# The sample tokens' depthwise convolution as products on GpSimd and sums on VectorE

## The chip, the cores and the metric
The kernel runs on one core of one Trainium2 chip. The metric is the device time of one execution in microseconds (us). A core has a matrix engine (TensorE, PE in the profile, with its weight loads as PEld), VectorE (DVE), ScalarE (ACT), GpSimd (POOL) and SyncE (SP), which here only issues DMAs. Each engine runs its own row of instructions strictly in order, and waits on semaphores for what other engines produce.

## The reference
One layer of a streaming encoder: a half-step SwiGLU feed-forward network, a mixer, a second half-step network, a norm. 1024 prompt tokens and 8 sample requests of 16 tokens pass through the same weights. The mixer projects each token once into q, k, v, eight forget logits and the two halves of a GLU:

```
z = h @ w_in                              # q | k | v | forget logits | conv GLU pair
q, k = rms(q) * g_q, rms(k) * g_k         # per head of 64
logf = log_sigmoid(fl + b_f)              # summed along time for the attention
u = a * sigmoid(gt)                       # 512 channels
y[t, c] = sum_j u_pad[t + j, c] * conv_w[j, c] + conv_b[c]     # 31 taps, causal
out = concat(attention(q, k, v, logf), silu(layernorm(y))) @ w_out
```

For the prompt, u_pad starts with 30 zeros; for each sample request it starts with 30 stored rows and has 16 new ones. The change concerns y of the 8 x 16 = 128 sample tokens alone.

## The kernel before
Channels lie on the 128 partitions, in four channel tiles (ct). For each of them, u[ct] holds 30 zeros and 1024 prompt columns, and behind them, as usv[ct], eight stretches of 46 columns, one for a request. acc[ct] has 1152 columns for y: 1024 of the prompt, 128 of the sample tokens. cw holds the 31 tap weights of each channel, convb (in vecs) the bias.

The mixer starts with the GLU: for each ct and each of three token chunks PE multiplies, ACT takes the sigmoid, DVE the product into u (the function glu). Then follows the projection, called the z stage here: six column blocks cb of 256 columns (the first with the 8 forget logits besides, 264), in the order v, v, k, k, q, q. A block takes nine tiles of 128 tokens, the sample tokens (tt = 8) first; a tile is 24 matmuls into a PSUM tile z. Weights come by DMA, are rounded on ACT (wh, L117), and the rest that was rounded off is taken on POOL (wl, L118); two such pieces belong to a block and are split two blocks ahead.

What happens to z of a tile depends on its block. In blocks 0 and 1 ACT copies it out; in block 0 DVE also adds the forget logits' bias (fl, L849). In blocks 2 to 5 ACT sums the squares of each head and takes the root, and DVE takes the reciprocal (rr, L858). In blocks 2 to 4 ACT copies z, POOL multiplies the copy by rr (L865), and for k by the gain as well (L869). In block 5 DVE multiplies z by rr straight from PSUM (L862). The sample rows stay on the chip as kts and qts, and PE transposes them five tiles later (q8T). z has six PSUM tiles in turn.

At the end of block 0 the log-sigmoid is computed for all tokens at once: two ACT operations and a chain of some twenty short DVE operations on 72 columns (ezq, L763 to L772, with lf as its result). In block 3, PE transposes lf, and DVE runs the cumulative sums as scans (nf L789; nfs L807, and L809 with 16 columns).

The convolution runs on DVE beside all this. The generator conv_taps goes through four ct of 31 taps; one step issues two operations: a tap on the prompt's 1024 columns, accumulated in PSUM (cv, L693 for the first tap, L696), and the same tap on the 128 sample columns, accumulated in acc (L694, L697). Five steps are taken after each GLU piece of ct 2 and 3, one or two after each tile of the z stage, the rest behind the loop.

PE's order is written by hand; the other engines' rows are ordered by a scheduler from the program's order, priorities and assumed costs. So code added at one place can shift instructions at many others. The attention, the layer norm, w_out and the second network follow the z stage.

Of the kernel before, what the change touches and what calls it, by code (L numbers as in the profile page):

```python
# [1 line left out]

# [10 lines left out]
ALU = mybir.AluOpType  # L13
AX = mybir.AxisListType
# [3 lines left out]
P = 128  # L18
D = 1024
KD = D // P  # L20
SEQ = 1024
NS = 8
TS = 16
# [9 lines left out]
CW = 31  # L33
# [10 lines left out]
def trunk_layer(  # L44
# [9 lines left out]
    pe, act, dve, pool_e, sp = nc.tensor, nc.scalar, nc.vector, nc.gpsimd, nc.sync  # L54
# [13 lines left out]
    def tmp(n, name="tmp", p=P):  # L68
        t = tp.tile([P, 768], F32, tag="tmp", name=name)
        return t[:p, :n]  # L70
# [7 lines left out]
    def defer(n, f):  # L78
        pending.append([n, f])

    def tick():
        for e in pending:
            e[0] -= 1
        due = [e for e in pending if e[0] <= 0]
        for e in due:
            pending.remove(e)
        for _, f in due:
            f()
# [91 lines left out]
    cw = const.tile([P, 4, CW], F32, name="cw")  # L180
# [9 lines left out]
    convb, lng, lnb = (vecs[:, 96 + 4 * i:100 + 4 * i] for i in range(3))  # L190
# [10 lines left out]
    def bank(name="b"):  # L201
        return ps.tile([P, 512], F32, tag="b", name=name, bufs=nb)
# [163 lines left out]
    def run(gen, n):  # L366
        for _ in range(n):
            if next(gen, "end") == "end":
                return False
        return True  # L370
# [274 lines left out]
    u = [up_.tile([P, ST + SEQ + NS * (ST + TS)], F32, tag=f"u{ct}", name=f"u{ct}") for ct in range(4)]  # L645
    acc = [up_.tile([P, NTOK], F32, tag=f"acc{ct}", name=f"acc{ct}") for ct in range(4)]
    usv = [t[:, ST + SEQ:].rearrange("p (s t) -> p s t", t=ST + TS) for t in u]
# [36 lines left out]

    def conv_taps():
        for ct in range(4):
            av = acc[ct][:, SEQ:].rearrange("p (s t) -> p s t", t=TS)
            cv = ps.tile([P, SEQ], F32, tag="cv", name="cv", bufs=1)
            for j in range(CW):
                w = cw[:, ct, j:j + 1]  # L690
                u0, u1 = u[ct][:, j:j + SEQ], usv[ct][:, :, j:j + TS]
                if j == 0:
                    dve.tensor_scalar(cv, u0, w, convb[:, ct:ct + 1], ALU.mult, ALU.add)  # L693
                    dve.tensor_scalar(av, u1, w, convb[:, ct:ct + 1], ALU.mult, ALU.add)  # L694
                else:
                    dve.scalar_tensor_tensor(cv if j < CW - 1 else acc[ct][:, :SEQ], u0, w, cv, ALU.mult, ALU.add)  # L696
                    dve.scalar_tensor_tensor(av, u1, w, av, ALU.mult, ALU.add)  # L697
                yield

    conv = conv_taps()  # L700

    def glu(ct, c, w0, w1):
        pa, pb = glu_mm(c, w0, w1)
        sg = tmp(C, "sg")
        act.activation(sg, pb[:, :C], AF.Sigmoid)
        n = C if c < 2 else 256
        dve.tensor_tensor(u[ct][:, ST + c * C:ST + c * C + n], pa[:, :n], sg[:, :n], ALU.mult)
        if c == 2:
            dve.tensor_tensor(
                usv[ct][:, :, ST:], pa[:, 256:C].rearrange("p (s t) -> p s t", t=TS),  # L710
                sg[:, 256:].rearrange("p (s t) -> p s t", t=TS), ALU.mult)
# [5 lines left out]
    for ct in range(2, 4):  # L717
        w = [ws.take(b_u + 2 * ct + i) for i in range(2)]
# [6 lines left out]
    def conv_states():  # L725
        t2 = tmp(DC, "us2")
        for ct in range(4):
            act.copy(t2[:, ct * P:(ct + 1) * P].rearrange("p (s t) -> p s t", t=TS), usv[ct][:, :, ST:])
        defer(2, lambda: conv_states_out(t2))
# [23 lines left out]
    def out_rows(flat, tt):  # L753
        return flat[0][tt * P:(tt + 1) * P] if tt < 8 else flat[1]

    def log_sigmoid():
        sh = [P, 72]
        x = fl.rearrange("p a b -> p (a b)")
        ezq = tmp(216, "ezq")
        e, z, q = (ezq[:, 72 * i:72 * i + 72] for i in range(3))  # L760
        act.activation(e, x, AF.Abs)
        act.activation(e, e, AF.Exp, scale=-1.0)
        dve.tensor_scalar(z, e, 2.0, None, ALU.add)  # L763
        dve.reciprocal(z, z)
        dve.tensor_tensor(z, z, e, ALU.mult)
        dve.tensor_tensor(e, z, z, ALU.mult)
        dve.tensor_scalar(q, e, 1.0 / 17, 1.0 / 15, ALU.mult, ALU.add)
        for d in (13, 11, 9, 7, 5, 3, 1):
            dve.tensor_tensor(q, q, e, ALU.mult)
            dve.tensor_scalar(q, q, 1.0 / d, None, ALU.add)  # L770
        dve.scalar_tensor_tensor(q, z, 2.0, q, ALU.mult, ALU.mult)
        dve.scalar_tensor_tensor(lf.rearrange("p a b -> p (a b)"), x, 0.0, q, ALU.min, ALU.subtract)  # L772
        sp.dma_start(f_prompt[0, 0].rearrange("(i p) h -> p i h", p=P), lf[:, 0:8, :])
        sp.dma_start(f_sample[0].rearrange("s t h -> (s t) h"), lf[:, 8, :])
# [41 lines left out]
    def sample_rows(cb):  # L816
        return (kts if cb < 4 else qts)[:, 2 * (cb % 2):2 * (cb % 2) + 2, :].rearrange("p a t -> p (a t)")

    def sample_t(cb):
        b = bank("q8T")  # L820
        dst = sample_rows(cb)
        for p in range(2):
            T(b[:, p * P:(p + 1) * P], dst[:, p * P:(p + 1) * P])
        if cb < 4:
            act.copy(dst, b[:, :256])
        else:
            act.activation(dst, b[:, :256], AF.Copy, scale=gqc)

    for cb, (c0, n) in enumerate(QKV):
        i0 = b_qkv + 2 * cb  # L830
        w = [ws.take(i0 + kq) for kq in range(2)]
        ws.split(i0 + 4)
        for tt in [8] + list(range(8)):
            c, o = divmod(tt, 3)
            b = bank("z")
            for kt in range(KD):
                a_h = hh[c][:, kt, o * P:(o + 1) * P]
                a_l = hl[c][:, kt, o * P:(o + 1) * P]
                wh, wl = (t[:, kt % 4, :] for t in w[kt // 4])
                pe.matmul(b[:, :n], lhsT=a_h, rhs=wh, start=kt == 0, stop=False)  # L840
                pe.matmul(b[:, :n], lhsT=a_h, rhs=wl, start=False, stop=False)
                pe.matmul(b[:, :n], lhsT=a_l, rhs=wh, start=False, stop=kt == KD - 1)
            cols = slice(c0 % DA, c0 % DA + 256)
            rows = slice(tt * P, (tt + 1) * P)
            t = sample_rows(cb) if tt == 8 and cb > 1 else tmp(256, "qkv")
            if cb < 2:
                act.copy(t, b[:, :256])
                if cb == 0:
                    dve.tensor_tensor(fl[:, tt, :], b[:, 256:264], bfb, ALU.add)  # L849
                sp.dma_start(out_rows(vflat, tt)[:, cols], t)  # L850
                sp.dma_start(vd[rows, cols], t)
            else:
                sq = up_.tile([P, DH], F32, tag="sq", name="sq", bufs=1)
                rr = up_.tile([P, 4], F32, tag="rr", name="rr", bufs=3)
                for h in range(4):
                    act.activation(sq, b[:, h * DH:(h + 1) * DH], AF.Square, accum_out=rr[:, h:h + 1])
                act.activation(rr, rr, AF.Sqrt, scale=1.0 / DH, bias=eps)
                dve.reciprocal(rr, rr)  # L858
                tv = t.rearrange("p (h d) -> p h d", h=4)
                rb = rr.unsqueeze(2).to_broadcast([P, 4, DH])  # L860
                if cb == 5:
                    dve.tensor_tensor(tv, b[:, :256].rearrange("p (h d) -> p h d", h=4), rb, ALU.mult)  # L862
                else:
                    act.copy(t, b[:, :256])
                    pool_e.tensor_tensor(tv, tv, rb, ALU.mult)  # L865
                if tt == 8:
                    defer(5, lambda cb=cb: sample_t(cb))
                if cb < 4:
                    pool_e.tensor_tensor(tv, tv, gkb.unsqueeze(1).to_broadcast([P, 4, DH]), ALU.mult)  # L869
                    sp.dma_start(out_rows(kflat, tt)[:, cols], t)  # L870
                if tt < 8:
                    sp.dma_start((kd if cb < 4 else qd)[rows, cols], t)
            run(conv, 1 + tt % 2)
            tick()
            if cb == 3:
                run(cum, 1)
        if cb == 0:
            log_sigmoid()
            conv_states()

    while run(conv, 1):
        pass

# [321 lines left out]
    for n in range(len(stages) + LAG):  # L1205
        q = {k: [] for k in "SBXY"}
        if n < len(stages):
            h, j = stages[n]
# [9 lines left out]
        if n >= LAG:  # L1218
            h, j = stages[n - LAG]
# [138 lines left out]
```

## Time and profile before
| | us |
|---|---|
| median of 3 runs | 2374.18 (2370.69 to 2375.71) |
| profiled execution, device time | 2371.12 |
| its span | 2369.4 |
| PE busy in the span | 2301.1 (97%) |
| DVE busy | 1240.5 (52%) |
| ACT busy | 654.3 (28%) |
| POOL busy | 532.9 (22%) |

The device time has 1.7 us outside the span. The busy shares are means over stages: in most of the program DVE is far from full, in the GLU and the z stage it isn't, which is to be read from windows of the trace. The z stage runs from 1044.7 to 1208.7 us. The granted clock of PE is 1.00 there. A row of the timeline gives start, duration, engine, source line, operation and the tiles it writes and reads; rows of the same kind that follow one another are put together (x17). Instructions of one engine that don't depend on each other overlap slightly, so the distance between two starts may be less than a duration.

### The profile page before, as it was taken

To read this page: it belongs to the slowest core of one execution; us is meant where nothing else is said; L and a number is where in the kernel's file an instruction comes from. 1 tells how busy PE (TensorE), PEld (TensorE's weight loads), DVE (VectorE), ACT (ScalarE), POOL (GpSimd) and SP (SyncE) were. 2 spreads that over 40 slices of the span, in tenths; PEclk is the share of its full clock that TensorE was granted. 3 is DMA by queue.
4 is the path that set the end of the run, shared out by engine and by line. 5 is a ranking of instruction groups with operands and counts; after the bars stand their busy time and mean duration, and the time that the engine had idled before them with its cause. 6 is when DMAs were issued, how large, how long until landed. Compare 5 with 4: busy or idle time off the path is not lost.

```text
span 2369.4 us, 34222 instructions
## 1 busy us (share of the span) xinstructions
PE 2301.1 (97%) x13923; PEld 2206.7 (93%) x13923; DVE 1240.5 (52%) x2349; ACT 654.3 (28%) x1426; POOL 532.9 (22%) x423
## 2 busy tenths in 40 slices
PE   7999999999999998999989999999999999999998
PEld 4799999999999998999977779899999999999998
DVE  3542343244333447899977887743443344423445
ACT  4411111111111114314567763431111111111112
POOL 1012111121121121212546650121121221121210
PEclk8999999999999999999999999999999999999999
DMA  8233323221111111124242320111111111111102
GB/s 307 88 108 118 112 91 107 89 63 45 36 47 44 36 48 51 38 63 134 76 127 82 110 90 27 45 49 41 36 46 45 37 54 36 36 54 36 42 22 81
DMA packets 165173, 165.75 MB, mean 70 GB/s; under 512 B 9855, under 2 KB 141867, under 8 KB 161937
## 3 DMA queue, kind: packets, MB, share of 16 engines
q1 hardware_dynamic: 165017, 163.57, 22.2%
q8 instruction: 110, 1.80, 0.3%
q14 instruction: 46, 0.38, 0.1%
HBM read 147.10 MB, written 16.68 MB: 69 GB/s over the span
## 4 chain that ended last, share of the span: by engine, by line
PE 83%; DVE 11%; DMA 2%; ACT 2%; issue 1%; POOL 0%; DVEq 0%; SPq 0%; ACTq 0%; POOLq 0%
PE ub L446 8%; PE ub L447 8%; PE ub L448 8%; PE ua L446 8%; PE ua L447 8%; PE ua L448 8%; PE d L446 8%; PE d L448 8%; PE d L447 8%; DVE cv L696 4%; PE pa L341 2%; DMA nfb<-nfd 1%; DVE acc L697 1%; PE wo L446 1%; PE wo L447 1%
## 5 line engine op out<-in xcount | busy, mean ns | idle before, releaser
L118 POOL TENSOR_TENSOR wl<-raw,wh 128x1024 fp32r<-128x1024 f32 (+1 forms) x152 | 368.0, 2429 | 1600.5 <-ACT wh L117 1482.8
L485 DVE TENSOR_TENSOR g<-ub,sg 128x384 f32<-128x384 f32 x132 | 73.5, 557 | 773.6 <-PE ub L448 755.0
L446 PE MATMUL ub<-hh,wh 128*128 128x384 f32 x1168 | 398.3, 341 | 3.6 <-ACT hh L430 3.6
L447 PE MATMUL ub<-hl,wh 128*128 128x384 f32 x1168 | 397.4, 340 | 1.0 <-DVE hl L431 1.0
L448 PE MATMUL ub<-hh,wl 128*128 128x384 f32 x1168 | 396.9, 340 | 0.0
L446 PE MATMUL ua<-hh,wh 128*128 128x384 f32 x1136 | 382.5, 337 | 2.3 <-ACT hh L441 2.0
L447 PE MATMUL ua<-hl,wh 128*128 128x384 f32 x1136 | 380.6, 335 | 1.2 <-DVE hl L442 0.6
L448 PE MATMUL ua<-hh,wl 128*128 128x384 f32 x1136 | 380.4, 335 | 0.0
L117 ACT CAST wh<-raw 128x1024 fp32r<-128x1024 f32 (+1 forms) x160 | 165.8, 1049 | 764.3 <-issue 452.8
L453 DVE SCALAR_TENSOR_TENSOR x<-d,hgate,x 128x384 f32<-128x384 f32 (+1 forms) x528 | 296.0, 570 | 128.7 <-PE d L448 122.9
L446 PE MATMUL d<-gh,wh 128*128 128x384 f32 x1056 | 356.9, 338 | 4.8 <-DVE t L429 4.7
L448 PE MATMUL d<-gh,wl 128*128 128x384 f32 x1056 | 356.9, 338 | 0.0
L447 PE MATMUL d<-gl,wh 128*128 128x384 f32 x1056 | 355.9, 337 | 0.0
L446 PEld LDWEIGHTS ub<-hh,wh 128*128 128x128 f32 x1168 | 221.0, 189 | 12.3 <-issue 5.0
L446 PEld LDWEIGHTS ua<-hh,wh 128*128 128x128 f32 x1136 | 213.6, 188 | 14.5 <-issue 7.5
L447 PEld LDWEIGHTS ub<-hl,wh 128*128 128x128 f32 x1168 | 221.2, 189 | 1.5 <-DVE hl L431 1.5
L448 PEld LDWEIGHTS ub<-hh,wl 128*128 128x128 f32 x1168 | 221.1, 189 | 0.0
L447 PEld LDWEIGHTS ua<-hl,wh 128*128 128x128 f32 x1136 | 213.8, 188 | 2.0 <-DVE hl L442 1.1
L448 PEld LDWEIGHTS ua<-hh,wl 128*128 128x128 f32 x1136 | 213.7, 188 | 0.0
L446 PEld LDWEIGHTS d<-gh,wh 128*128 128x128 f32 x1056 | 199.0, 188 | 12.0 <-DVE t L429 5.0
L447 PEld LDWEIGHTS d<-gl,wh 128*128 128x128 f32 x1056 | 198.8, 188 | 0.0
L448 PEld LDWEIGHTS d<-gh,wl 128*128 128x128 f32 x1056 | 198.6, 188 | 0.0
(263 smaller groups left out, 3183.1 us busy)
## 6 DMA issues: line engine op xcount, KB each, us to landing
raw<-in_w_up_dram SPq DMA_DIRECT2D x88, 512.0 KB
araw<-in_w_ada_dram SPq DMA_DIRECT2D x24, 1024.0 KB
raw<-in_w_down_dram SPq DMA_DIRECT2D x44, 512.0 KB
raw<-in_w_in_dram SPq DMA_DIRECT2D x18, 512.0 KB
abulk<-in_w_ada_dram SPq DMA_DIRECT2D x4, 1536.0 KB
out_dram<-yo SPq DMA_DIRECT2D x18, 256.0 KB
out_dram<-qkv SPq DMA_DIRECT2D x34, 128.0 KB
araw<-in_w_ada_dram SPq DMA_DIRECT2D x8, 512.0 KB
```

The lines of the kernel that those rows point to most:

```text
L117: act.copy(hi[:, :a * b], raw)
L118: self.sub.tensor_sub(lo[:, :a * b], raw, r32(hi[:, :a * b]))
L341: pe.matmul(pa[32 * i:32 * i + 32, :], lhsT=cst32[:, k, :], rhs=raw, start=first, stop=last)
L446: pe.matmul(out, lhsT=wh, rhs=mh_, start=first, stop=False)
L447: pe.matmul(out, lhsT=wh, rhs=ml_, start=False, stop=False)
L448: pe.matmul(out, lhsT=wl, rhs=mh_, start=False, stop=last)
L453: dve.scalar_tensor_tensor(xs[:, :n], b[:, :n], gate[:, dt, 0:1], xs[:, :n], ALU.mult, ALU.add)
L485: dve.tensor_tensor(g32, pb[:, :C], sg, ALU.mult)
L696: dve.scalar_tensor_tensor(cv if j < CW - 1 else acc[ct][:, :SEQ], u0, w, cv, ALU.mult, ALU.add)
L697: dve.scalar_tensor_tensor(av, u1, w, av, ALU.mult, ALU.add)
```

## The change
conv_taps keeps the prompt's taps only. A second generator, conv_sample, computes the sample tokens. For each ct it takes two requests at a time: POOL multiplies, for each of the 2 x 16 tokens, a window of 31 columns by the 31 weights (128 x 992 products, tensor_tensor), into a buffer wn; DVE sums the 31 products of each token with one tensor_reduce into 32 columns of acc. After the four pairs of a ct, POOL adds the bias to the 128 columns. wn is the front of acc[3], which the prompt's taps fill only with their last one; there is one wn, so a product waits for the sum before it and a sum for its product. Products and sums are kept in program order. One product is issued after every second tile from block 1 on, what is left behind the loop. In all 4 + 120 DVE operations go, and 16 products, 16 sums and 4 additions of the bias come. Line numbers shift by 1 before the convolution, and by 12 to 16 behind it.

```
     def conv_taps():
         for ct in range(4):
-            av = acc[ct][:, SEQ:].rearrange("p (s t) -> p s t", t=TS)
             cv = ps.tile([P, SEQ], F32, tag="cv", name="cv", bufs=1)
             for j in range(CW):
                 w = cw[:, ct, j:j + 1]
-                u0, u1 = u[ct][:, j:j + SEQ], usv[ct][:, :, j:j + TS]
+                x = u[ct][:, j:j + SEQ]
                 if j == 0:
-                    dve.tensor_scalar(cv, u0, w, convb[:, ct:ct + 1], ALU.mult, ALU.add)
-                    dve.tensor_scalar(av, u1, w, convb[:, ct:ct + 1], ALU.mult, ALU.add)
+                    dve.tensor_scalar(cv, x, w, convb[:, ct:ct + 1], ALU.mult, ALU.add)
                 else:
-                    dve.scalar_tensor_tensor(cv if j < CW - 1 else acc[ct][:, :SEQ], u0, w, cv, ALU.mult, ALU.add)
-                    dve.scalar_tensor_tensor(av, u1, w, av, ALU.mult, ALU.add)
+                    dve.scalar_tensor_tensor(cv if j < CW - 1 else acc[ct][:, :SEQ], x, w, cv, ALU.mult, ALU.add)
                 yield
 
+    def conv_sample():
+        wn = acc[3][:, :2 * TS * CW].rearrange("p (s t j) -> p s t j", s=2, j=CW)
+        for ct in range(4):
+            w = cw[:, ct].unsqueeze(1).unsqueeze(1).to_broadcast([P, 2, TS, CW])
+            av = acc[ct][:, SEQ:].rearrange("p (s t) -> p s t", t=TS)
+            for s0 in range(0, NS, 2):
+                win = usv[ct][:, s0:s0 + 2, 0:TS].unsqueeze(3).to_broadcast([P, 2, TS, CW])
+                win = replace(win, ap=[*win.ap[:3], (1, CW)])
+                tc.keep_in_program_order(pool_e.tensor_tensor(wn, win, w, ALU.mult))
+                yield
+                tc.keep_in_program_order(dve.tensor_reduce(av[:, s0:s0 + 2], wn, AX.X, ALU.add))
+            pool_e.tensor_scalar(acc[ct][:, SEQ:], acc[ct][:, SEQ:], convb[:, ct:ct + 1], None, ALU.add)
+
     conv = conv_taps()
+    convs = conv_sample()
...
             run(conv, 1 + tt % 2)
+            if cb > 0 and tt % 2:
+                run(convs, 1)
             tick()
...
+    while run(convs, 1):
+        pass
     while run(conv, 1):
         pass
```

How the rows move is shown at three places. In them acc_7425 to acc_7428 are acc[0] to acc[3], and u_7421 to u_7424 are u[0] to u[3], so acc_7428 as an output of 128x992 is wn.

First POOL at the end of block 0 and ahead of block 2, before:

```order
L118 TENSOR_TENSOR wl<-raw,wh 128x1024 x4
L991 MEMSET room_10595 128x128
L118 TENSOR_TENSOR wl<-raw,wh 128x1024 x2
L865 TENSOR_TENSOR kts<-kts,rr 128x256
L869 TENSOR_TENSOR kts<-kts,gkb 128x256
```

and after:

```order
L119 TENSOR_TENSOR wl<-raw,wh 128x1024 x4
L706 TENSOR_TENSOR acc_7428<-u_7421,cw 128x992 x4
L1007 MEMSET room_10507 128x128
L709 TENSOR_SCALAR acc_7425<-acc_7425,vecs 128x128
L706 TENSOR_TENSOR acc_7428<-u_7422,cw 128x992
L119 TENSOR_TENSOR wl<-raw,wh 128x1024 x2
L877 TENSOR_TENSOR kts<-kts,rr 128x256
L881 TENSOR_TENSOR kts<-kts,gkb 128x256
```

Five of the sixteen products now stand between the splits of block 0 and those two of block 1, ahead of the first multiply of block 2.

Next DVE from the last fl of block 0 on, before:

```order
L849 TENSOR_TENSOR fl<-z,bfb 128x8
L696 SCALAR_TENSOR_TENSOR cv<-u_7422,cw,cv 128x1024
L697 SCALAR_TENSOR_TENSOR acc_7426<-u_7422,cw,acc_7426 128x128
L696 SCALAR_TENSOR_TENSOR cv<-u_7422,cw,cv 128x1024
L763 TENSOR_SCALAR ezq<-ezq 128x72
L697 SCALAR_TENSOR_TENSOR acc_7426<-u_7422,cw,acc_7426 128x128
L764 RECIPROCAL ezq<-ezq 128x72
L696 SCALAR_TENSOR_TENSOR cv<-u_7422,cw,cv 128x1024
L765 TENSOR_TENSOR ezq<-ezq 128x72
```

and after:

```order
L861 TENSOR_TENSOR fl<-z,bfb 128x8
L695 SCALAR_TENSOR_TENSOR cv<-u_7422,cw,cv 128x1024 x2
L775 TENSOR_SCALAR ezq<-ezq 128x72
L708 TENSOR_REDUCE acc_7425<-acc_7428 128x32
L776 RECIPROCAL ezq<-ezq 128x72
L695 SCALAR_TENSOR_TENSOR acc_7426<-u_7422,cw,cv 128x1024
L777 TENSOR_TENSOR ezq<-ezq 128x72
L708 TENSOR_REDUCE acc_7425<-acc_7428 128x32
L778 TENSOR_TENSOR ezq<-ezq 128x72
L693 TENSOR_SCALAR cv<-u_7423,cw,vecs 128x1024
L779 TENSOR_SCALAR ezq<-ezq 128x72
L708 TENSOR_REDUCE acc_7425<-acc_7428 128x32
```

Where a small tap stood between two large ones, sums stand now, the first five of them within the ezq chain, a tap or less apart.

Last, DVE at the end of block 4 and the start of block 5, before:

```order
L858 RECIPROCAL rr<-rr 128x4
L697 SCALAR_TENSOR_TENSOR acc_7428<-u_7424,cw,acc_7428 128x128
L862 TENSOR_TENSOR qts<-z,rr 128x256
L696 SCALAR_TENSOR_TENSOR cv<-u_7424,cw,cv 128x1024
L697 SCALAR_TENSOR_TENSOR acc_7428<-u_7424,cw,acc_7428 128x128
L858 RECIPROCAL rr<-rr 128x4
L696 SCALAR_TENSOR_TENSOR acc_7428<-u_7424,cw,cv 128x1024
```

and after:

```order
L695 SCALAR_TENSOR_TENSOR cv<-u_7424,cw,cv 128x1024 x2
L870 RECIPROCAL rr<-rr 128x4
L695 SCALAR_TENSOR_TENSOR cv<-u_7424,cw,cv 128x1024
L708 TENSOR_REDUCE acc_7428<-acc_7428 128x32
L870 RECIPROCAL rr<-rr 128x4
L695 SCALAR_TENSOR_TENSOR acc_7428<-u_7424,cw,cv 128x1024
L874 TENSOR_TENSOR qts<-z,rr 128x256
```

The last sum and the last large tap stand ahead of the multiply that makes qts, where before that multiply stood ahead of the last two large taps.

## Rows read from the trace of the kernel before

**Rows 1.** The chain that ended last, by engine, share of the span.
```profile
PE 83%; DVE 11%; DMA 2%; ACT 2%; issue 1%; POOL 0%; DVEq 0%; SPq 0%; ACTq 0%; POOLq 0%
```

**Rows 2.** Busy time of each engine by stretch (count), granted clock, DMA share, GB/s.
```profile
1077.30:1140.00 62.70, 59.75 (x498) 58.93 (x499) 62.70 (x105) 32.77 (x146) 23.45 (x25) 1.00 0.44 130
1140.00:1198.70 58.70, 58.20 (x491) 57.68 (x490) 58.69 (x104) 34.50 (x192) 21.94 (x28) 1.00 0.18 59
```

**Rows 3.** Waits of PE from 980 to 1216: total, times, longest.
```profile
PE cs L251 <- ACT us L728: 2.2, 2, 1.4
...
PE z L840 <- DVE nf L789: 0.9, 1, 0.9
PE z L840 <- DVE rr L858: 0.5, 1, 0.5
```

**Rows 4.** Busy time of line L697 alone, by stretch.
```profile
1077.30:1198.70 121.40, 27.56 (x64) 1.00 0.31 96
```

**Rows 5.** DVE's groups by form: busy us, mean ns; idle before.
```profile
L696 DVE SCALAR_TENSOR_TENSOR cv<-u,cw,cv 128x1024 f32<-128x1024 f32 x116 | 148.0, 1276 | 0.0
...
L697 DVE SCALAR_TENSOR_TENSOR acc<-u,cw,acc 128x128 f32<-128x128 f32 x120 | 53.1, 452 | 0.0
...
L1026 DVE TENSOR_REDUCE sst<-sS 128x1 f32<-128x272 f32 x8 | 3.4, 425 | 0.0
```

**Rows 6.** POOL's groups by form, with two inputs.
```profile
L118 POOL TENSOR_TENSOR wl<-raw,wh 128x1024 fp32r<-128x1024 f32 x150 | 363.1, 2428 | 1580.2 <-ACT wh L117 1462.5 <-PE pa L341 117.7
...
L865 POOL TENSOR_TENSOR qkv<-qkv,rr 128x256 f32<-128x256 f32 x24 | 15.4, 644 | 38.1 <-DVE rr L858 38.1
L869 POOL TENSOR_TENSOR qkv<-qkv,gkb 128x256 f32<-128x256 f32 x16 | 11.8, 737 | 1.3
L903 POOL TENSOR_TENSOR lna<-lna,lnq 128x384 f32<-128x384 f32 x9 | 9.9, 1098 | 14.5 <-ACT lnq L902 14.1
```

**Rows 7.** Timeline at the end of block 0, PE, POOL, DVE: start, duration.
```profile
1070.69 0.28 PE L842 MATMUL z<-wh,hl 128*128 128x264 f32 x1
1070.74 4.83 POOL L118 TENSOR_TENSOR wl<-raw,wh 128x1024 fp32r<-128x1024 f32 x2 [22.43 <-ACT wh L117]
...
1077.19 0.16 DVE L849 TENSOR_TENSOR fl<-z,bfb 128x8 f32<-128x8 f32 x1
1077.32 1.29 DVE L696 SCALAR_TENSOR_TENSOR cv<-u,cw,cv 128x1024 f32<-128x1024 f32 x1
1078.51 0.35 DVE L697 SCALAR_TENSOR_TENSOR acc<-u,cw,acc 128x128 f32<-128x128 f32 x1
1078.77 1.28 DVE L696 SCALAR_TENSOR_TENSOR cv<-u,cw,cv 128x1024 f32<-128x1024 f32 x1
```

**Rows 8.** Timeline from 982 to 991, POOL and DVE.
```profile
982.56 2.40 POOL L118 TENSOR_TENSOR wl<-raw,wh 128x1024 fp32r<-128x1024 f32 x1 [38.08 <-ACT wh L117]
982.67 2.63 DVE L694 TENSOR_SCALAR acc<-u,cw,vecs 128x128 f32<-128x128 f32 x2 [4.15 <-ACT u L677]
...
985.22 4.54 DVE L697 SCALAR_TENSOR_TENSOR acc<-u,cw,acc 128x128 f32<-128x128 f32 x17
...
987.20 4.84 POOL L118 TENSOR_TENSOR wl<-raw,wh 128x1024 fp32r<-128x1024 f32 x1 [2.24 <-ACT wh L117]
```

**Rows 9.** Timeline at the first rr and multiply of block 2.
```profile
1100.15 4.81 POOL L118 TENSOR_TENSOR wl<-raw,wh 128x1024 fp32r<-128x1024 f32 x2 [22.05 <-ACT wh L117]
...
1110.85 0.17 DVE L858 RECIPROCAL rr<-rr 128x4 f32<-128x4 f32 x1
...
1111.10 0.61 POOL L865 TENSOR_TENSOR kts<-kts,rr 128x256 f32<-128x256 f32 x1 [6.14 <-DVE rr L858]
```

**Rows 10.** Timeline in block 5: qts, the last large tap, the transposes, the last z.
```profile
1194.94 0.41 DVE L862 TENSOR_TENSOR qts<-z,rr 128x256 f32<-128x256 f32 x1
...
1196.82 1.24 DVE L696 SCALAR_TENSOR_TENSOR acc<-u,cw,cv 128x1024 f32<-128x1024 f32 x1
1196.85 0.38 PE L251 MATMUL q8T<-ident,qts 128*128 128x128 f32 x2
...
1208.37 0.28 PE L842 MATMUL z<-wh,hl 128*128 128x256 f32 x1
```

More of the change, by code (lines that the diff above doesn't have):

```diff
@@ L1 @@
 from contextlib import ExitStack
+from dataclasses import replace
 import concourse.bass as bass
```

## The prediction
> **What bounds the kernel now.** I read the chain that ended last first. Over the whole program it is PE's, 83% of the span, with DVE second at 11% [rows 1]; so a change to the convolution counts only where PE waits for DVE. Next come the busy times by stretch. From 1077.3 to 1198.7 us, five of the six column blocks of the query/key/value projection, DVE is busy without a gap (62.70 of 62.70, then 58.69 of 58.70), and PE idles 2.95 and 0.50 us of it [rows 2]. PE's waits show which idle time that is: 2.2 us for the sample states' copies, 0.9 us for a scan and 0.5 us for an rr, 3.6 us together; the last two are DVE's own and the first hangs on DVE's queue too [rows 3]. So two engines are full in one stretch. PE ends it at 1208.65 (last z matmul at 1208.37 for 0.28); DVE ends its last large tap at 1198.06 [rows 10]. All PE can gain in this stage is those 3.6 us. What it can lose is set by how late DVE hands over rr, scans and, in the last block, qts.
>
> **What is removed.** In the stretch DVE runs 64 of the 120 small sample taps, 27.56 us busy [rows 4]. A normal one starts at 1078.51 and frees the queue at 1078.77, 0.26 us for a row of 0.35 us [rows 7], so 64 of them return 27.56 - 64 x 0.08 = 22.4 us of queue, the two first taps of a channel tile some 0.5 us more: 22.9. The other 56 lie before 1077.3. What they free there is mostly not kept: in DVE's order the addition of the forget logits of block 0 (fl) waits for PE's z, and nothing behind it can pass. PE's last z of block 0 ends at 1070.97, while DVE adds the last fl only at 1077.19 [rows 7]. After the change DVE reaches it at about 1071.2, so it is 6.0 us early, and no more than that. Five large taps also move ahead of this fl (70 stand behind it in the order before, 65 after), at 1.19 us of queue each (1077.32 to 1078.51) [rows 7]: 6.0 us.
>
> **What is added on DVE.** Sixteen sums of 992 elements per partition. No row shows that form. The nearest above and below are the large tap, 1276 ns for 1024 elements, and the small one, 0.34 us in its ordinary rows for 128: 1.045 ns an element, hence 1.24 us busy and some 1.15 us of queue. The only reduction in the trace, 425 ns for 272 elements [rows 5], gives 1.55 us if all of it were per element. I take 1.15, since the reduction's row lies close under the taps' line (0.49 us for 272): 16 x 1.15 = 18.4 us; the other end is 24.8. Taps now follow each other directly 17 times with the result of one read by the next. Rows overlap by 0.09 us now (1.28 us rows, 1.19 us apart); if a dependent tap loses that, it is 1.5 us, else 0. I take 1.5. Up to here DVE's stretch is shorter by 22.9 + 6.0 + 6.0 - 18.4 - 1.5 = 15.0 us.
>
> **What is added on POOL, and the waits.** Sixteen products of 992 elements with two inputs. The nearest POOL rows with two inputs are the weights' split, 2428 ns for 1024 elements (2.37 ns each), and the layer norm's sum, 1098 ns for 384 (2.86 ns) [rows 6]. That is 2.35 to 2.84 us; I take 2.4, as the split is nearly of the same size. The 16 x 2.4 = 38.4 us fit into POOL, which is busy for 45.4 of the stretch's 121.4 us [rows 2]. But they are not beside DVE's work, because there is one buffer: product k+1 waits for sum k, and both are pinned in order. DVE's queue stops at each sum whose product isn't there, and everything behind it (taps, rr, scans) stops with it.
> First the five products ahead of block 2. POOL can start them only behind the two splits that run from 1070.74 to 1075.57 [rows 7]. From there one cycle is 2.4 + 1.15 + two handovers of about 0.1 (an rr that ends at 1111.02 starts POOL at 1111.10 [rows 9]), 3.8 us: the fifth sum ends at 1094.5, 23.3 us behind fl. In that time DVE's row holds six taps (7.2), ten short ezq operations (2.4) and five sums (5.75), 15.4 us. The wait is about 8 us.
> Then the other eleven. Each product stands in POOL's row behind a multiply by rr that itself waits for DVE, or behind a pair of them; from that rr to the product's end are 0.1 + 0.64 + 0 to 0.74 + 2.4 = 3.1 to 3.9 us [rows 6]. On DVE one or two taps (1.2 to 2.5 us) stand between rr and the sum; one product also has two splits ahead of it. I take 1.9 us each: 21 us. If POOL ran far ahead it would be 0; if every one met a split, 11 x 4.
> Last, DVE operations with both inputs in SBUF that meet a running product. Before the change, while a split ran from 982.56 to 984.96, two small first taps of 128 elements took 2.63 us; and while 17 small taps ran for 4.54 us, a split that began among them took 4.84 us in place of 2.43 [rows 8]. So each stops the other. The small tap's mean of 452 ns against its ordinary 350 shows how rare and long such stops are [rows 5]. The ezq chain and the sixteen 16-wide scans are of that form and now stand among products and splits. About four stops of 2.4 us: 9.5 us; 0 if they happen to miss.
> Waits together: 8 + 21 + 9.5 = 38.5 us, against 15.0 saved. The last tap moves from 1198.06 by 23.5 to 1221.6.
> [...]
>
> **What this does to PE.** Three places hand it on. The first rr of block 2 comes behind the five sums and the ezq chain, near 1115 in place of 1110.85; the scan in block 3 for which PE waits 0.9 us now comes later by some 6 us. Both only delay PE inside the stage. In block 5 DVE computes qts from PSUM at 1194.94, ahead of the last tap; PE transposes it at 1196.85 and needs 11.8 us more to the stage's end [rows 10]. In the new order the last tap stands ahead of that operation. So the stage ends at 1221.6 + 0.41 (qts) + 0.15 (handover) + 11.8 = 1234.0, against 1208.65: +25.3 us. Earlier delays of PE are inside this sum, since DVE ends last. What follows starts from that end in the same order: nothing is given back. PE's first 2.2 us of waiting go, and are lost again here.
> The profiled execution took 2371.12 us, of which 2369.4 are the span; with 25.3 it is 2396.4. The median of the runs shown is 2374.18, 3.1 above the profiled one; on it the forecast is 2399.5, put as 2400. Each 0.3 us on the product, or on the sum, is about 4.8 us.
>
> **Rivals.**
> A: the waits are hidden and PE is the bound. Then 3.6 us of PE's idle time go: 2370.6 on the median. For it speaks the 15.0 us taken from DVE and POOL's free 76 us. Its place is the qts operation of block 5: PE isn't held if the waits stay under 38.5 - 25.3 = 13 us. Against it: the first five products alone cost 8, in one buffer with nothing else to do on DVE. This is the faster side.
> B: only that first stretch and half the later waits come, as when POOL's multiplies are early and the two-input stops miss: 8 + 10.5 + 4 = 22.5 us, 16 less than taken, a stage later by 9: about 2384.
> C: the product has the layer norm's rate, 2.84 us, and the sums the upper bound of 1.55: 16 x 0.44 + 16 x 0.4 = 13.4 us more, 2413; the product alone 2407.
> D: POOL is late with the weights' splits, since up to two products stand ahead of them, and PE waits for wl. The two splits of 1100.15 end at 1104.96 now, and the next rr of the sample tokens is at 1110.85 [rows 9]; but in the new order PE is later as well. A split late by a product or two costs at most 5 us, inside the range of the forecast.
> E: the change doesn't do what it says, if products were all left to the end. The order shows them spread over blocks 1 to 4, so under 1 in 100.
>
> **How the numbers follow.** The forecast with the errors of its terms (2391 to 2407) has 0.56, B (2379 to 2391) 0.21, C with what lies above 2407 0.12, A 0.06, and a draw, B and A in between, 0.05. A measurement tells this kernel from no change beyond about 0.2%, 4.7 us: faster 0.06, same 0.06, slower 0.88. The range reaches over B's upper part to C's product and sum: 2382 to 2413.
>
> **What will show it.** Right: DVE idle in front of the sums for POOL, 5 to 10 us in 1074 to 1095 and 1 to 3 us at most of the later ones; product rows of 2.4 us, sums of 1.2; single ezq operations near 2 us; PE waiting for kts, the scan and most of all qts; the last tap near 1222 and the last z matmul near 1234. Wrong: sums that start without a wait, a DVE with gaps for PE's z in blocks 2 to 4, a last z before 1210. If the products take 1.2 us or less, or POOL runs ahead of DVE after all, A holds and the forecast falls.

## The result: slower by 0.9%, and the profile after

| | before | after |
|---|---|---|
| median of the runs, us | 2374.94 (4 runs) | 2394.99 (4 runs) |
| profiled execution, us | 2371.12 | 2396.06 |
| its span, us | 2369.4 | 2394.2 |
| z stage, first z matmul to the end of the last, us | 164.0 (1044.7 to 1208.7) | 183.7 (1046.2 to 1229.9) |
| end of the last large tap, us | 1198.06 | 1216.10 |

The ratio of after to before is 1.0089, with a 95% interval from 1.0077 to 1.010. By the medians that is 20 us; forecast were 25, in a range of 8 to 39. The two profiled executions lie 24.9 us apart, of which the z stage makes 19.7.

First the busy times by stretch, in the columns of [rows 2] (PE, PEld, DVE, ACT, POOL, granted clock, DMA share, GB/s), of the kernel after:

```profile
1077.30:1140.00 62.70, 57.74 (x485) 57.04 (x485) 58.53 (x70) 28.14 (x126) 34.98 (x29) 1.00 0.38 116
1140.00:1200.00 60.00, 50.92 (x394) 49.96 (x394) 48.98 (x63) 28.08 (x155) 37.90 (x38) 0.91 0.20 67
```

DVE was full there before; now it is not, 15 us of gaps in 122.7, and PE, which lost 3.5 us before, loses 14. An engine has got free and the stage has got longer: the mark of waits, not of work. PE's waits within the z stage of the kernel after (total, times, longest) give six rows where [rows 3] has three:

```profile
PE q8T L252 <- POOL qts L877: 5.8, 1, 5.8
PE q8T L252 <- DVE qts L874: 3.8, 1, 3.8
PE q8T L252 <- POOL kts L881: 2.5, 1, 2.5
PE z L852 <- DVE nf L801: 2.5, 1, 2.5
PE q8T L252 <- DVE rr L870: 1.9, 1, 1.9
PE z L852 <- DVE nfs L819: 1.3, 1, 1.3
```

17.8 us together. Behind 12 of them is a late DVE, and behind that DVE's own wait, in the same view of DVE:

```profile
DVE acc L708 <- POOL acc L706: 18.2, 10, 3.4
```

Ten of the sixteen sums (L708) stood and waited for their product (L706). What the two operations took, by their lines (minimum, median, maximum in ns, first and last start):

```profile
L706 POOL TENSOR_TENSOR acc<-u,cw x16: 2142/2168/2220, 1076.9 to 1211.4; 128x992 f32<-128x992 f32 x16
```
```profile
L708 DVE TENSOR_REDUCE acc<-acc x16: 1166/1186/1187, 1079.1 to 1213.6; 128x32 f32<-128x992 f32 x16
```

The longest of PE's waits, 5.8 us for the qts of block 4, has another cause. DVE had the rr of that tile ready at 1179.31 (a row of 0.17 from 1179.14), but POOL came to qts only at 1183.58, 4.3 us later, because its row was full:

```profile
1177.78 2.36 POOL L119 TENSOR_TENSOR wl<-raw,wh 128x1024 fp32r<-128x1024 f32 x1
1180.09 0.62 POOL L877 TENSOR_TENSOR qkv<-qkv,rr 128x256 f32<-128x256 f32 x1
1180.78 0.72 POOL L881 TENSOR_TENSOR qkv<-qkv,gkb 128x256 f32<-128x256 f32 x1
1181.46 2.15 POOL L706 TENSOR_TENSOR acc<-u,cw 128x992 f32<-128x992 f32 x1
1183.58 0.61 POOL L877 TENSOR_TENSOR qts<-qts,rr 128x256 f32<-128x256 f32 x1
```

Then the start of the first products at the end of block 0, where [rows 7] stood. POOL's timeline after (start, duration, engine, line, operation):

```profile
1072.18 4.77 POOL L119 TENSOR_TENSOR wl<-raw,wh 128x1024 fp32r<-128x1024 f32 x2 [22.43 <-ACT wh L118]
1076.90 2.14 POOL L706 TENSOR_TENSOR acc<-u,cw 128x992 f32<-128x992 f32 x1
1080.35 2.17 POOL L706 TENSOR_TENSOR acc<-u,cw 128x992 f32<-128x992 f32 x1 [1.30 <-DVE acc L708]
```

and DVE's over the same time:

```profile
1073.18 0.16 DVE L861 TENSOR_TENSOR fl<-z,bfb 128x8 f32<-128x8 f32 x1
1073.31 2.62 DVE L695 SCALAR_TENSOR_TENSOR cv<-u,cw,cv 128x1024 f32<-128x1024 f32 x2
1075.83 1.18 DVE L775 TENSOR_SCALAR ezq<-ezq 128x72 f32<-128x72 f32 x1
1079.08 1.19 DVE L708 TENSOR_REDUCE acc<-acc 128x32 f32<-128x992 f32 x1 [2.07 <-POOL acc L706]
1080.18 0.59 DVE L776 RECIPROCAL ezq<-ezq 128x72 f32<-128x72 f32 x1
...
1081.79 0.81 DVE L777 TENSOR_TENSOR ezq<-ezq 128x72 f32<-128x72 f32 x1
1082.55 1.19 DVE L708 TENSOR_REDUCE acc<-acc 128x32 f32<-128x992 f32 x1
```

The cycle is seen at once: the product at 1076.90, its sum at 1079.08, the next product only at 1080.35, 1.30 us after POOL was ready for it, then the next sum at 1082.55. It is 3.45 us long; 3.8 were forecast. The second sum shows no wait of its own, because the small ezq operation ahead of it has already stood still for the product: 0.81 us for an operation that takes 0.22 where POOL is idle (L778 at 1083.65).

The end of the stage, where [rows 10] stood, in DVE's timeline after:

```profile
1213.59 1.19 DVE L708 TENSOR_REDUCE acc<-acc 128x32 f32<-128x992 f32 x1 [1.59 <-POOL acc L706]
1214.70 0.17 DVE L870 RECIPROCAL rr<-rr 128x4 f32<-128x4 f32 x1
1214.82 1.28 DVE L695 SCALAR_TENSOR_TENSOR acc<-u,cw,cv 128x1024 f32<-128x1024 f32 x1
1216.01 0.42 DVE L874 TENSOR_TENSOR qts<-z,rr 128x256 f32<-128x256 f32 x1
```

and in PE's:

```profile
1216.57 0.41 PE L252 MATMUL q8T<-ident,qts 128*128 128x128 f32 x2 [3.84 <-DVE qts L874]
```

Last sum, last tap, qts, transposes: the order of the forecast, with PE standing 3.84 us at its end.

### The profile page after: what moved, and what is told of

Same layout as the page of the kernel before. It is cut to its first block, busy times and chain, and to the rows that moved or that the text cites. A ratio compares the mean times of both kernels' runs of the same rounds, so it can differ in the third digit from the quotient of the medians.

```text
span 2394.2 us, 34106 instructions
## 1 busy us (share of the span) xinstructions
PE 2311.2 (97%) x13923; PEld 2215.3 (93%) x13923; DVE 1229.9 (51%) x2241; ACT 654.0 (27%) x1426; POOL 565.6 (24%) x443
## 4 chain that ended last, share of the span: by engine, by line
PE 84%; DVE 8%; POOL 2%; DMA 2%; ACT 2%; issue 2%; SPq 0%; DVEq 0%; POOLq 0%; ACTq 0%
PE ub L447 9%; PE ub L448 9%; PE ub L449 9%; PE ua L447 8%; PE ua L449 8%; PE ua L448 8%; PE d L447 8%; PE d L449 8%; PE d L448 7%; PE pa L342 2%; DVE cv L695 2%; DMA nfb<-nfd 1%; PE wo L447 1%; PE wo L448 1%; PE wo L449 1%
## 5 line engine op out<-in xcount | busy, mean ns | idle before, releaser
L118 ACT CAST wh<-raw 128x1024 fp32r<-128x1024 f32 (+1 forms) x160 | 165.8, 1049 | 764.5 <-issue 473.5
```

The costliest lines, as they stand in the source:

```text
L118: act.copy(hi[:, :a * b], raw)
```

## The experiments

Nine kernels ran, each timed beside the kernel before. Ratios are to it, with 95% intervals.

**e1, no sample convolution.**
```
-                tc.keep_in_program_order(pool_e.tensor_tensor(wn, win, w, ALU.mult))
                 yield
-                tc.keep_in_program_order(dve.tensor_reduce(av[:, s0:s0 + 2], wn, AX.X, ALU.add))
-            pool_e.tensor_scalar(acc[ct][:, SEQ:], acc[ct][:, SEQ:], convb[:, ct:ct + 1], None, ALU.add)
+            pool_e.memset(acc[ct][:, SEQ:], 0.0)
```


> Leaves out the sample tokens' convolution altogether: no products, no sums; the 128 sample columns of acc are set to zero, so the sample outputs are not the reference's. The prompt's taps stay. This is the bound of what any way of computing the sample tokens can reach. Theory (the loss is DVE standing still in front of products that are late): 2371 us, the 3.6 us of PE's idle time before go and PE alone bounds the projection. Rival A (the dependent taps that now follow each other directly, and the changed order, cost by themselves): at least 2380. Rival B (POOL's multiplies and splits are late behind the products): 2371 as well.

Measured: 2367.85 us, 0.9975 (0.9963 to 0.9986), 3 us below the theory's 2371. PE has no wait in the z stage, which takes 159.2 us. So the sample tokens cost the kernel before some 6 us, and as long as the rest of the kernel stays as it is, another way of computing them can hardly save more. DVE's waits also show how much room there is:

```profile
DVE rr L868 <- ACT rr L867: 27.8, 12, 2.7
```

DVE waits 27.8 us for PE's pace, 25.6 of them within the z stage; that is more than the 16 sums need (16 x 1.10 us of queue = 17.6).

**e2, sums without products.**
```
-                tc.keep_in_program_order(pool_e.tensor_tensor(wn, win, w, ALU.mult))
+                if ct == 0 and s0 == 0:
+                    pool_e.memset(acc[3][:, :2 * TS * CW], 0.0)
```


> Leaves out the 16 products: the buffer is zeroed once on POOL and DVE sums it 16 times, so the sample outputs are the bias alone. The 16 sums cost DVE the same, but none waits for a product, and no product stops the ezq chain or the scans. Theory (waits): the 18 us in front of sums and some 10 us of stops go, the last large tap comes near 1188 in place of 1216, PE is the bound: 2371 to 2374 us. Rival A (the sums' and dependent taps' own DVE time is the loss): 2385 or more. Rival B (POOL's multiplies are late behind products): 2371 to 2374 as well.

Measured: 2369.93 us, 0.9987 (0.9976 to 0.9998), 1 us below the theory's range. The z stage has no PE wait here either. This experiment's rival A, that the sums' own time is the loss, has fallen.

**e3, products without sums.**
```
-                tc.keep_in_program_order(dve.tensor_reduce(av[:, s0:s0 + 2], wn, AX.X, ALU.add))
...
-            pool_e.tensor_scalar(acc[ct][:, SEQ:], acc[ct][:, SEQ:], convb[:, ct:ct + 1], None, ALU.add)
+            pool_e.memset(acc[ct][:, SEQ:], 0.0)
```


> Leaves out the 16 sums (the sample columns of acc are zeroed): the products stay at their places on POOL, one behind the other without waiting for DVE. Theory (DVE's waits at sums): no wait in front of sums; stops of the ezq chain and the scans remain, some 10 us, but DVE has 18 us of sums less: 2371 to 2374 us. Rival B (products in POOL's row make the multiplies for kts and qts and the splits late, whatever DVE does): most of the loss stays, 2385 or more.

Measured: 2380.88 us, 1.0031 (1.0022 to 1.0041). The theory as it stood said 2371 to 2374, so it was not the whole. Without a single sum, the products cost 7 us against before and 13 against e1. PE's waits in the z stage of e3 are these, foremost:

```profile
PE q8T L252 <- POOL qts L876: 3.4, 1, 3.4
PE q8T L252 <- POOL qkv L876: 3.2, 1, 3.2
```

Both name POOL. Its busy time at the change from block 2 to block 3 (the stretch, POOL's busy us and count, PE's clock, DMA):

```profile
1123.00:1145.20 22.20, 21.30 (x19) 0.97 0.39 114
```

There two splits, four products and thirteen multiplies by rr or gkb fill POOL's row to 96%. The multiplies that make kts stand behind them, and PE transposes kts at 1144.37, at the end of the wait of 3.2 us. Two more of e3's waits are DVE's, for buffers that a product still reads or writes (4.3 us at a memset of a room, 2.9 at the last tap); they belong to this experiment.

The four cells together, against e1's 0.9975: the sums alone +0.0012, the products alone +0.0056, both, as in the change, +0.0114. More than half of the loss comes with the products alone or the sums alone; the rest, 0.0046 or some 11 us, only where both are there and each waits for the other.

**e4, without the pins.**
```
-                tc.keep_in_program_order(pool_e.tensor_tensor(wn, win, w, ALU.mult))
+                pool_e.tensor_tensor(wn, win, w, ALU.mult)
...
-                tc.keep_in_program_order(dve.tensor_reduce(av[:, s0:s0 + 2], wn, AX.X, ALU.add))
+                dve.tensor_reduce(av[:, s0:s0 + 2], wn, AX.X, ALU.add)
```


> The changed kernel without the pins: products and sums may move, and the scheduler puts all 16 of them into the GLU's time, ahead of the projection's end of block 0, where DVE has gaps (37.5 of 40 us busy from 1020 to 1060). Theory: sums wait for products there too, but fewer of the waits lie in the stretch in which DVE holds PE, and qts is no longer behind a late tap: 2371 to 2380 us. Rival A (the sums' own DVE time): 2390 as with the pins, since DVE has as much to do up to the last tap. Rival B (POOL's row): splits of the first blocks stand behind products, PE waits for wl at the start of the projection: 2385 to 2395, with waits of PE for wl.

Measured: 2384.56 us, 1.0038 (1.0024 to 1.0051): less than half of the loss, but above the theory's range. PE's first wait and DVE's first wait in the trace of e4:

```profile
PE cs L252 <- ACT us L740: 9.8, 2, 8.5
```
```profile
DVE acc L708 <- POOL acc L706: 16.7, 13, 2.3
```

The scheduler has moved all products and sums ahead of the last fl of block 0; DVE waits nearly as long as with the pins (16.7 against 18.2 us), falls behind there, and adds the last fl at 1086.94 in place of 1073.18. PE pays mostly in one place: the transposes of the conv states, behind ACT, which first needs fl. So the pins decide where the waits are paid, not whether they come. That PE would wait for wl (rival B here) is not seen.

**e5, half products.**
```
-                tc.keep_in_program_order(pool_e.tensor_tensor(wn, win, w, ALU.mult))
+                if ct == 0 and s0 == 0:
+                    pool_e.memset(acc[3][:, :2 * TS * CW], 0.0)
+                tc.keep_in_program_order(pool_e.tensor_tensor(wn[:, :1], win[:, :1], w[:, :1], ALU.mult))
```


> Each product covers one request in place of two (128x496, about 1.09 us in place of 2.17); the other half of the buffer is zeroed once, so every second request's sample outputs are the bias alone. Places, order rules and the 16 sums of 992 elements stay. Theory, now in two parts (DVE stands at sums for products, and products make POOL's row too full around the splits; both scale with a product's length): by the forecast's 4.8 us for 0.3 us of product, 1.08 us are worth 17 us: 2378 us, between 2373 and 2382. Rival (the handing over between the engines and the order of the rows cost by themselves, the product's length hardly): 2388 or more.

Measured: 2381.35 us, 1.0029 (1.0017 to 1.0041), 0.0060 or 14 us below the change, where 17 were worked out from the forecast's slope. The half product took 1.18 us and not 1.09, which makes those 17 some 16. So most of the loss goes with the products' length.

**e6, the buffer as two halves.**
```
-                tc.keep_in_program_order(pool_e.tensor_tensor(wn, win, w, ALU.mult))
+                for o in range(2):
+                    tc.keep_in_program_order(pool_e.tensor_tensor(wn[:, o:o + 1], win[:, o:o + 1], w[:, o:o + 1], ALU.mult))
                 yield
-                tc.keep_in_program_order(dve.tensor_reduce(av[:, s0:s0 + 2], wn, AX.X, ALU.add))
+                for o in range(2):
+                    tc.keep_in_program_order(dve.tensor_reduce(av[:, s0 + o:s0 + o + 1], wn[:, o:o + 1], AX.X, ALU.add))
```


> The one buffer is used as two halves: 32 products and 32 sums of one request each (128x496), so that POOL may refill the first half while DVE sums the second. The computation is whole. Theory that the single buffer's to and fro is the larger part of the waits: a cycle falls from 3.4 us (2.17 + 1.10 + handovers) to about 2.9, and 16 x 0.5 = 8 us of waits go: 2385 to 2389. Rival (POOL's row of splits, multiplies and products is the limit, the buffer isn't): 2393 to 2398, since the products are as long together and stand at the same places.

Measured: 2392.39 us, 1.0079 (1.0065 to 1.0092). It lies between the theory's range and the rival's, 0.6 us from the rival's. Its interval and the change's overlap; by the ratios 2.4 us come back, where 8 were expected. DVE's wait in e6:

```profile
DVE acc L710 <- POOL acc L707: 17.4, 20, 3.4
```

17.4 us in twenty places, where the change has 18.2 in ten. POOL waits for no sum any more (the first eight half products run in one row of 9.10 us from 1074.43), but the sum still stands as close behind its product, and DVE waits on. The halves are also longer than the whole, which the expectation left out: two products take 2.36 us in place of 2.17, two sums 1.18 us of queue in place of 1.10. By the forecast's slope that is some 4 us more, so by that estimate the one buffer is worth some 7 us of the loss; e6 doesn't separate the two.

**e7, spread over other blocks.** The sum is issued at the tile in which DVE comes to it, not by the generator:
```
+    slots = [0, 2, 4, 6, 36, 38, 40, 42, 44, 45, 46, 47, 48, 49, 50, 51]
+    prods = {s: k for k, s in enumerate(slots)}
+    sums = {(s + 2 if s < 44 else s + 1): k for k, s in enumerate(slots)}
...
+            gi = 9 * cb + (tt + 1) % 9
...
+                if gi in sums:
+                    sample_sum(sums[gi])
...
+            if gi in prods:
+                sample_prod(prods[gi])
             run(conv, 1 + tt % 2)
-            if cb > 0 and tt % 2:
-                run(convs, 1)
```
sample_prod(k) and sample_sum(k) are the pinned product and sum of the change; the sum stands behind fl (block 0) or behind the multiply by rr (blocks 4 and 5) of its tile.

> The same products and sums, computed whole, at other places: four in block 0, five in block 4 and seven in block 5 of the projection, where POOL has no split and no second multiply, none beside the ezq chain of block 1 nor in the k blocks 2 and 3; each sum is pinned behind the fl or rr of a later tile, so that its product is done when DVE comes to it. The last large tap comes behind the last sum, and behind qts. Theory (waits and POOL's full row at these places, not the work itself): hardly a wait in front of a sum, PE is the bound, 2368 to 2372 us, faster than before by 3 to 6 us. Rival A (the sums' and products' own time costs wherever they stand): 2385 or more. Rival C (the end of block 5 is now too full: the last tap and what the attention waits for come late): 2376 to 2385, with PE waiting for DVE or POOL behind the last z.

Measured: 2378.28 us, 1.0016 (1.0007 to 1.0025), in rival C's range, not the theory's. The z stage takes 159.1 us without a PE wait, as expected. That DVE would hardly wait at sums was a miss:

```profile
DVE acc L713 <- POOL acc L708: 14.2, 9, 2.3
```

These nine waits, nearly as much as in the change, lie at the end, from 1176.9 us on, where of the large taps only the last is still to come. There they hold up no z tile, but the q tiles. Behind the z stage PE waits for kp (before: 2.65 us):

```profile
PE kT L252 <- DMA kp<-kd: 8.6, 1, 8.6
```
```profile
1209.38 0.43 SPq L1101 DMA_DIRECT2D qp<-qd  x1
1209.86 0.65 SPq L1101 DMA_DIRECT2D kp<-kd  x1
```

In SP's timeline kp is issued at 1209.86, 4.5 us after the last z, because SP's row first issues the DMA of a q tile that DVE makes at 1208.56, behind a sum that waited for its product. From the end of block 4 on each of eight tiles in a row has a product, and its sum stands one tile behind it; through the one buffer a cycle takes 3.45 us, and a tile of PE 2.85.

**e8, the sum two tiles behind its product.** As e7, with slots in a regular step from block 2 on:
```
+    slots = list(range(18, 50, 2))
+    prods = {s: k for k, s in enumerate(slots)}
+    sums = {s + 2: k for k, s in enumerate(slots)}
```


> The same 16 products and sums, computed whole, one buffer; from block 2 on a product behind the multiplies of every second tile, its sum pinned behind the rr of two tiles later (so some 5.7 us after it). So the to and fro of one buffer is taken away, while products still stand among POOL's multiplies and splits in the k blocks, and none beside the ezq chain. Theory in two parts: DVE hardly waits at sums; where the splits stand with products (ends of blocks 2 and 3) POOL's row stays full and makes kts, qts or rr's multiplies late: 2372 to 2380 us. Rival (the to and fro is all of it): 2367 to 2371. Rival (work itself, dependent taps): 2388 or more.

Measured: 2376.78 us, 1.0014 (1.0005 to 1.0024). DVE's waits at sums, PE's first wait in the z stage, and POOL's busy time in block 2:

```profile
DVE acc L713 <- POOL acc L708: 3.9, 4, 1.7
```
```profile
PE q8T L252 <- POOL qts L889: 3.6, 1, 3.6
```
```profile
1110.00:1140.00 30.00, 28.66 (x30) 1.00 0.35 115
```

With the same buffer, the same pins on product and sum and most products still in blocks 2 to 4, the wait at sums falls from 18.2 to 3.9 us and 0.0075 of the 0.0089 go. What is left of the theory's second part is POOL's row, full to 96% in block 2 and late with qts in block 4; the z stage takes 165.6 us, 6.4 more than in e1.

**e9, spread with every second tile in block 5.** As e7, but also with four products in the GLU's time, and with every sum of the z stage two tiles behind its product:
```
+    slots = [-1, -2, -3, -4, 0, 2, 4, 6, 36, 38, 40, 42, 44, 46, 48, 50]
...
+    sums = {(s + 2 if s >= 0 else -100): k for k, s in enumerate(slots)}
...
             glu(ct, c, *w)
+            g = 3 * (ct - 2) + c
+            if 0 < g < 5:
+                sample_sum(g - 1)
+            if g < 4:
+                sample_prod(g)
             run(conv, 5)
```


> As e7, but in block 5 only every second tile has a product, so that DVE's qkv multiplies, and the DMAs behind them on SP, keep PE's pace: four products in the GLU's time, four in block 0, eight over blocks 4 and 5. e7's projection had no PE wait left, and lost behind it, where kp was issued 4 us late behind the DMAs of q. Theory: those 4 us come back: 2367 to 2372 us, faster than before by 2 to 7 us. Rival (the stages behind the projection lose in any case when the sums end late, by the last tap and the rooms' DMAs): 2376 to 2381, as e7. Rival (sums in the GLU's time make the last fl late, as without pins): PE waits for cs, 2375 to 2383.

Measured: 2369.87 us, 0.9982 (0.9973 to 0.9992): faster than before by 4 us, and than the change by 25, with the same 16 products and 16 sums. DVE's waits at sums, and PE's largest wait from the z stage to 1250:

```profile
DVE acc L713 <- POOL acc L708: 1.4, 2, 1.0
```
```profile
PE kT L252 <- DMA kp<-kd: 5.1, 1, 5.1
```

kp is issued at 1206.01 here, 0.5 us after the last z, and e1, without any sample work, waits 5.0 us for it too. Between e9 and e1 lie 0.0007, inside both intervals.

## Why the prediction was right, and where its steps were off

The direction held, and the mechanism in the main: PE is hurt by a DVE that stands in its row in front of sums, and the end is set by the last tap ahead of qts. Beside it works POOL's own full row, which the forecast had only as rival D; PE's longest wait, for the qts of block 4, is not among the three places that it named. The size was 25 us forecast, 20 measured. Step by step:

| step | forecast, us | measured, us | from |
|---|---|---|---|
| last fl of block 0, earlier | 6.0 | 4.0 | 1077.19 and 1073.18 |
| 16 sums, of queue | 18.4 | 17.6 | 1079.08 to 1080.18, x16 |
| dependent taps | 1.5 | 2.4 | 2.52 for two in place of 2.38, x17 |
| waits in the first five cycles | 8 | 6.8 | 2.07 at the sum, 4.7 in five ezq stops |
| waits at the other eleven sums | 21 | 16.1 | 18.2 less 2.07 |
| other two-engine stops | 9.5 | 6.9 | 2.1 in ezq, 4.8 in the short scans |
| last tap, later | 23.5 | 18.0 | 1198.06 and 1216.10 |
| qts to the stage's end | 11.8 | 13.3 | 1216.57 to 1229.91 |
| end of the stage, later | 25.3 | 21.3 | 1208.65 and 1229.91 |

With the 22.9 and 6.0 us of taps that go (as forecast), the measured terms give 16.9 for the last tap; 18.0 are seen; 1.1 us are not placed. The z stage began 1.5 us later (1046.2 against 1044.7), and this is already in the 4.0 of the first row: against PE's last z of block 0 the last fl came 5.5 us earlier, near the 6.0. The terms missed partly against each other, and that the two profiled executions lie 24.9 us apart, next to the 25.3 of the forecast, is chance.

The largest miss is the product, 2.17 us (2168 ns at the median) where 2.4 was taken from the split: eleven later waits, each shorter by 0.23 us or more, explain about half of the 5 us that the waits at those sums came out short.

The stops were near the size and at the places forecast, but more kinds of operation stop than the text said. L775, a tensor_scalar with a single input, took 1.18 us beside a split and product against 0.19 where POOL is idle (L782 at 1096.02); the short scans took 2.62 and 2.65 us for two beside a product (at 1158.75 and 1169.08), and 0.38 and 0.61 without one (at 1154.72 and 1164.81). [rows 8] had shown it already: the two small first taps there are a tensor_scalar, not an operation with both inputs in SBUF, as the forecast reads them. A sum didn't stop: in the kernel after one ran its usual 1.19 us beside a split of the usual 2.40:

```profile
1134.66 1.19 DVE L708 TENSOR_REDUCE acc<-acc 128x32 f32<-128x992 f32 x1 [1.04 <-POOL acc L706]
```
```profile
1134.59 2.40 POOL L119 TENSOR_TENSOR wl<-raw,wh 128x1024 fp32r<-128x1024 f32 x1
```

One step of the reasoning was too narrow: "because there is one buffer". In e6 POOL waits for no sum, and 2.4 us came back, some 7 by the estimate that allows for the longer halves; e8 kept the one buffer and lost most of the waits, 3.9 us in place of 18.2. What makes DVE wait is first how close behind its product a sum stands in the row, a tap or less in the first five, one or two taps in the others. The one buffer carries the delay on to the next product, and where products follow at every tile, as in e7's block 5, its cycle of 3.45 us sets the pace. What a wait costs depends on what stands behind it: e7's 14.2 us cost the z stage nothing.

A part was judged too small. Rival D, POOL being late because of the products, was put inside the forecast's range, and as a matter of the splits alone. e3 shows that the products by themselves cost 13 us against e1, through kts, qts and qkv multiplies that stand behind splits and products in a full row. In the change itself these waits and DVE's overlap. Two of PE's waits there carry POOL's name: of the 5.8 us for qts 4.3 are POOL's full row, while kts was multiplied 0.1 us after its rr, so its 2.5 us are DVE's. And DVE's two longest waits at sums, 3.4 and 3.1 us, are for products that stand behind a pair of splits in the same row (the splits at 1134.59 and 1138.31, at 1174.73 and 1177.78). How much of the whole loss is POOL's row can't be split from the traces of the change; e8, with prompt sums and a full row, still loses 0.0014 against before.

What stood in no step is PE's clock. In the kernel after, behind the wait for qts and behind the last one (stretch, PE busy, granted clock, DMA):

```profile
1180.00:1190.00 10.00, 5.76 (x29) 0.66 0.12 41
1215.00:1220.00 5.00, 3.43 (x18) 0.69 0.18 61
```

The granted clock fell from 1.00 to 0.66 and 0.69 as a mean of these stretches; in windows of 1 us it is 0.50 from 1184 to 1189 and from 1217 to 1220, and 1.00 again from 1190 and from 1221 on. Before these falls PE had stood for 5.8 and 3.8 us. A third one, 0.50 from 1149 to 1152, came behind a wait of 1.9 us, while behind the two of 2.5 us, which ended at 1115.74 and 1139.60, the clock stayed at 1.00; so the trace shows no length of wait from which it falls. The stage is 24.6 us longer than in e9 (183.7 against 159.1); 17.8 are waits, and for the other 6.8 the trace shows slower matmuls (0.21 us from start to start at 1185 to 1189, 0.12 from 1189.63 on): PE's busy time in the stage is 165.8 us, and 159.2 in e9 for as many matmuls. What of it lies ahead of the last tap cost no time by itself, if DVE and POOL set that tap's end, as argued above; the last piece shows: 13.3 us in place of 11.8 from the transposes to the stage's end.

Rival A, PE as the bound, is what e1, e2 and e9 show, at 0.9975 to 0.9987 (forecast for it: 3.6 us less). Its condition was that the waits stay below 13 us; e9's are 1.4, and even e7's 14.2 didn't reach PE within the stage.

Open: the stages from the last z to w_out differ between kernels by some us that no wait explains in full (191.2 us in e1, 191.6 before, 194.5 after, 197.3 in e2). These are single executions, and those of one kernel lie up to 5.5 us apart (2370.69 to 2376.23 before), as much as the two profiled executions lie further apart than the medians; nothing here tells why.

## What to carry to other kernels

Work that is moved to an idle engine isn't beside the old work if the result is asked for at once: look in the order at what stands between the operation and its consumer, and compare it with the operation's length; then look at who needs what stands behind the consumer. Free time on an engine is to be read where the work would stand, not over the stage; POOL was 37% busy in the stage before (45.4 of 121.4 us, [rows 2]), and 96% where e3's and e8's products stood. And an order that holds two engines together is best tied to a third event that comes late enough, here the rr of a later tile.

## What the runs showed of the hardware that was not expected

A tensor_reduce of 992 elements per partition in groups of 31 took 1.186 us, 1.2 ns an element, no more than a large tap (1276 ns for 1024, [rows 5]). A product on POOL whose windows overlap and whose weights are repeated took 2.17 us for 992, 2.19 ns an element, less than the split with its 2.37; half of it, 496 elements, took 1.18 us, more than half the time, so cutting a product in two costs 0.19 us. Two taps in a row, the second reading the first's result, start 1.31 us apart (1135.77 and 1137.08) in place of 1.19 ([rows 7]). And behind waits of 5.8, 3.8 and 1.9 us PE ran at a granted clock of 0.50 for 3 to 5 us, but not behind two of 2.5: beside 17.8 us of waits, PE's busy time grew by 6.6 us.
